# Another order of a recurrence step's pieces on TensorE

## The chip, the core and the metric

The kernel runs on one core of a Trainium2 chip. The metric is the device time of one execution in microseconds (us); a median over runs is given beside the time of the one execution that the profiler recorded. TensorE does the matrix products, VectorE, ScalarE (ACT) and GpSimd the elementwise work, SyncE (SP) issues the DMAs.

## The reference, cut to what matters

One step of a hybrid decoder layer over 1040 prompt rows (16 meta rows in front) and 64 sample rows. The input projection feeds two branches; the RWKV branch, whose work the change reorders, is a recurrence over time:

```python
def _rwkv7_step(S, inp):
    r, w, k, v, kk, a = inp
    sa = jnp.einsum('bhvk,bhk->bhv', S, -kk)
    S = S * w[:, :, None, :] + sa[..., None] * (kk * a)[:, :, None, :] + v[..., None] * k[:, :, None, :]
    return S, jnp.einsum('bhvk,bhk->bhv', S, r)

z = _rms_norm(x, lp['pre1']) @ lp['w_in']            # columns of the RWKV branch, the mLSTM branch, the gates
S_T, y = lax.scan(_rwkv7_step, S0, (r, decay, k, v, kk, a))
merged = ga * (ya @ p_a) + gb * (yb @ p_b)
h = x + _rms_norm(merged @ w_out, post1)
out = h + _rms_norm(jnp.square(jax.nn.relu(_rms_norm(h, pre2) @ w_ff_up)) @ w_ff_down, post2)
```

All products are in float32, the large ones as three products of rounded halves (hi*hi, hi*lo, lo*hi).

## The kernel before

The recurrence is computed in chunks of 64 rows. Four pairs of heads (j) times six groups (g) of three chunks make 24 steps; the last group of a pair holds two prompt chunks and the 64 sample rows. A group passes through four stages, one step each, so that in step i stage a works on group i, stage b on i-1, stage c on i-2 and stage d on i-3. Each stage is a generator that is cut into pieces by `yield`:

- Stage a (lines 637 to 757, six pieces) prepares the chunk: norms and gates (L651 to L667), the scaled keys (L673 to L702, on VectorE, ScalarE and GpSimd), the product L708 with X1, nd and its round trip through DRAM (L716 to L721, NR), values (L726, L727), the product L738 with MB, and bonus and gate (L746 to L756).
- Stage b (six pieces) inverts a triangular matrix. Its first piece is VectorE's alone: a chain of fifteen rounds of a product and a sum on small tiles (L766, L768), which reads NR, and then XC (L770). Pieces two to six each begin with a small product on TensorE (L778, L784, L794, L801, L807) and end with VectorE's reading of it (L780, L786, L796, L803; L811 with ScalarE's L810).
- Stage c (five pieces, seven with the sample rows) carries the state. Piece one forms GH and MR (L820 to L832). Pieces two, three and four multiply a chunk's GH with the state into pS, which has a single PSUM bank, and VectorE scales it into the next state St (L894); the chunk's output product follows one piece later. Piece five copies the output (L912). With the sample rows the products of L859 to L922 are added, and an order's entries 'e' call two more pieces.
- Stage d (four pieces) normalizes the output: a small product (L623, L946), eight Newton operations on VectorE (`newton`, lines 172 to 184), then scaling and the store.

TensorE also computes the input projection for later work in blocks of 72 matmuls (L283, L285, L287; three column tiles of 414, 414 and 276), the fill. `run_step` (L962) writes TensorE's order: it walks through a list of (stage, weight), calls that stage's next piece, and then pulls so many fill matmuls that their count follows the sum of the weights; a step's units are 72, or 144 in the last group of the first three head pairs. Entries of stages that have no work in a step are dropped with their weights. What stays of a stage at the end is run out, with two fill matmuls behind each piece.

`ORDER` serves 19 full steps (three of them with the sample rows, entries 'e' counted), three without stage a at the start of a new pair of heads, and three at the end. `ORDER_B` serves step 1 alone, in which only stages a and b have work, and `ORDER_A` step 0 and stage a by itself at a new pair. TensorE's order is kept as written (`manual_schedule`, L565). The order on VectorE, ScalarE, GpSimd and SyncE is laid down by the framework's planner when the program is built, from the order of the program and from when it takes an operation to be ready; each of these engines then runs its own queue in that order.

Of the kernel before, what the change touches and what calls it, by code (L numbers as in the profile page):

```python
# [102 lines left out]
def tile_hybrid_trunk_step(ctx, tc, x_prompt, x_sample, st_S, st_shift, st_C, st_n, st_m, st_conv,  # L103
# [210 lines left out]
    def blocks(n):  # L314
        drain()
        for _ in range(n):
            pull(1)
            drain()
# [56 lines left out]
    with banks(s=4, m=2), ExitStack() as st:  # L375
# [91 lines left out]
        with tc.manual_schedule(engines={mybir.EngineType.Activation, mybir.EngineType.PE}):  # L467
# [5 lines left out]
            for i in range(9):  # L473
# [6 lines left out]
                if i in CASTS:  # L480
                    b = first[len(w_first)]
# [473 lines left out]
        dma(out=yscr[j][:, GC * g + y0 - 64:GC * g + GC - 64], in_=yo[:, :ny])  # L955
        yield

    ORDER = (('c', 7), ('a', 0), ('c', 7), ('b', 3), ('c', 6), ('a', 6), ('c', 0), ('c', 9), ('d', 1), ('a', 0), ('b', 8), ('b', 4), ('b', 3), ('d', 0), ('a', 0), ('b', 6), ('e', 4), ('d', 0), ('e', 10), ('a', 0), ('b', 8), ('a', 0))
    ORDER_B = (('c', 6), ('a', 0), ('p', 68), ('b', 0), ('c', 15), ('c', 6), ('d', 0), ('a', 11), ('c', 0), ('c', 2), ('b', 0), ('a', 0), ('b', 7), ('b', 1), ('b', 4), ('d', 0), ('a', 0), ('e', 4), ('a', 0), ('b', 15), ('a', 1), ('e', 10), ('d', 0))
    ORDER_A = (('a', 39), ('a', 3), ('a', 6), ('a', 0), ('a', 7), ('a', 13))  # L960

    def run_step(gens, order, units, smp=False):  # L962
        todo = [(x, w) for x, w in order if x in gens or x == "p" or (x == "e" and smp)]
        tot = sum(w for _, w in todo)
        did = acc_ = 0
        for x, w in todo:
            next(gens.get("c" if x == "e" else x, iter(())), None)
            acc_ += w
            want = units * acc_ // tot
            pull(want - did)  # L970
            did = want
        for x in "dcba":
            for _ in gens.get(x, ()):
                pull(2)
# [9 lines left out]
    for i in range(NS + 3):  # L984
# [5 lines left out]
        if i >= NS:  # L990
            run_step(gens, ORDER, 72 * (i < NS + 2), i == NS + 1)
            continue
        j, g = steps[i]
        if g == 0 and j:
            mix_all()
            queue.pop(0)
            run_step(gens, ORDER, 72)
            blocks(0)
            mix_all()
            queue.pop(0)  # L1000
            run_step({"a": stage_a(j, g, sts[j, g])}, ORDER_A, 72 * FILLS[0])
        else:
            gens["a"] = stage_a(j, g, sts[j, g])
            run_step(gens, ORDER_A if i == 0 else ORDER_B if i == 1 else ORDER, 72 * (FILLS[g] + (g == 5) * (1 if j == 3 else 2)), g == 1 and j > 0)
            while g == 5 and j < 3 and (live or queue[0]):
# [174 lines left out]
    for c0 in (0, 5):  # L1180
        ps = sbank()
        for c in range(c0, c0 + 5):
            a, n = CH[c]
            nc.tensor.transpose(ps[:n, 68 * (c - c0):68 * (c - c0) + 68], E2[:, a:a + n], ident[:68, :68])
        for c in range(c0, c0 + 5):
            a, n = CH[c]
# [354 lines left out]
    for m in range(8):  # L1541
# [7 lines left out]
        for a, n in O_TILES:  # L1549
# [4 lines left out]
            e = min(a + n, 1024)  # L1554
# [466 lines left out]
```

## Time and profile before

| | |
|---|---|
| runs | 2024.83, 2026.06, 2026.5 us; median 2026.06 |
| profiled execution | 2024.88 us, its span 2023.0 us |
| TensorE matmuls busy | 1928.6 us (95%) |
| TensorE weight loads busy | 1747.6 us (86%) |
| VectorE busy | 1292.1 us (64%) |
| ScalarE, GpSimd busy | 795.6 us, 619.2 us |
| the 24 recurrence steps | about 84 to 840 us of the span |

The profile is that of one execution. Its engines are PE (TensorE's matmuls), PEld (its weight loads), DVE (VectorE), ACT (ScalarE), POOL (GpSimd) and SP (SyncE). A matmul's duration holds its way through the array, so that matmuls overlap: two fill matmuls start about 0.18 us apart and last 0.35 us each. An idle time in brackets is counted from the modelled end of the one before.

### The profile page before, as it was taken

The page shows a single profiled execution, that of the slowest core. Times are in us where ns is not written, and L with a number is a line of the kernel's source. Part 1 is how long each engine was busy: PE and PEld are TensorE (multiplying, and loading weights), DVE is VectorE, ACT ScalarE, POOL GpSimd, SP SyncE. Part 2 cuts the span into 40 slices and gives each one's busy share as a digit, 9 for nine tenths or more (in the row PEclk, how much of TensorE's full clock was granted, in tenths as well). Part 3 has the DMA queues.
Part 4 walks back from the last instruction along what each step waited for, and adds up shares of the span by engine and source line. Part 5 has one row for each costly group of instructions (what it writes and reads, how often), then busy time and mean ns, then how long its engine had stood idle before and what let it go on. Part 6 is the DMA issues. An engine that isn't in the chain of part 4 may idle for free. (4 is left out here: it accounts for less than half of the span.)

```text
span 2023.0 us, 35063 instructions
## 1 busy us (share of the span) xinstructions
PE 1928.6 (95%) x13163; PEld 1747.6 (86%) x13163; DVE 1292.1 (64%) x3464; ACT 795.6 (39%) x1841; POOL 619.2 (31%) x816
## 2 busy tenths in 40 slices
PE   8999999999999999999899998999999999999996
PEld 8988888888888888999788886999999978888875
DVE  6367668867767787487766539764334326666658
ACT  6434334433434343355565324453443442222212
POOL 3311221221122112252533305444444312222225
PEclk9989999999999999889999999999999999999998
DMA  5122112212111122132666614322333362222212
GB/s 162 53 69 72 52 46 68 66 47 69 64 54 58 58 66 71 49 110 82 221 193 201 214 56 149 119 94 87 103 114 97 123 226 86 87 87 88 95 59 88
DMA packets 163193, 197.43 MB, mean 98 GB/s; under 512 B 22060, under 2 KB 125542, under 8 KB 163024
## 3 DMA queue, kind: packets, MB, share of 16 engines
q1 hardware_dynamic: 163024, 195.19, 30.0%
q8 instruction: 104, 1.70, 0.3%
q14 instruction: 65, 0.53, 0.1%
HBM read 139.80 MB, written 55.10 MB: 96 GB/s over the span
## 5 line engine op out<-in xcount | busy, mean ns | idle before, releaser
L207 POOL TENSOR_TENSOR lo<-raw,hi 128x128 fp32r<-128x128 f32 (+1 forms) x528 | 327.4, 654 | 807.8 <-ACT hi L200 762.5
L283 PE MATMUL g<-u,hi 128*128 128x414 f32 (+4 forms) x1120 | 382.7, 342 | 1.9 <-ACT gst L533 1.1
L287 PE MATMUL g<-u,lo 128*128 128x414 f32 (+4 forms) x1120 | 383.6, 342 | 0.0
L285 PE MATMUL g<-u,hi 128*128 128x414 f32 (+4 forms) x1120 | 381.5, 341 | 0.0
L1930 DVE TENSOR_TENSOR ACC<-g,ACC 128x512 f32<-128x512 f32 x234 | 159.2, 689 | 118.0 <-PE g L221 118.0
L283 PEld LDWEIGHTS g<-u,hi 128*128 128x128 f32 x1120 | 215.9, 193 | 7.4 <-issue 1.5
L287 PEld LDWEIGHTS g<-u,lo 128*128 128x128 f32 x1120 | 215.9, 193 | 5.1 <-POOL lo L207 0.3
L285 PEld LDWEIGHTS g<-u,hi 128*128 128x128 f32 x1120 | 215.7, 193 | 3.8 <-issue 0.2
L219 PE MATMUL g<-hi,ah 128*128 128x512 f32 (+1 forms) x515 | 202.8, 394 | 2.4 <-ACT ah L1886 2.4
L220 PE MATMUL g<-lo,ah 128*128 128x512 f32 (+1 forms) x515 | 203.4, 395 | 0.9 <-POOL lo L207 0.8
L221 PE MATMUL g<-hi,ah 128*128 128x512 f32 (+1 forms) x515 | 202.7, 394 | 0.4 <-DVE ah L1887 0.2
L200 ACT CAST hi<-raw 128x1024 fp32r<-128x1024 f32 x98 | 102.5, 1047 | 68.4 <-PE g L285 18.5
L1886 ACT CAST ah<-hr 128x1088 fp32r<-128x1088 f32 x32 | 34.0, 1103 | 220.5 <-PE g L220 217.0
L1823 PE MATMUL g<-T,op 128*128 128x272 f32 x416 | 120.3, 289 | 0.0
L1821 PE MATMUL g<-T,op 128*128 128x272 f32 x416 | 120.2, 289 | 0.0
L1822 PE MATMUL g<-T,op 128*128 128x272 f32 x416 | 120.0, 289 | 0.0
L219 PEld LDWEIGHTS g<-hi,ah 128*128 128x128 f32 x515 | 97.0, 188 | 25.7 <-ACT ah L1886 2.8
L220 PEld LDWEIGHTS g<-lo,ah 128*128 128x128 f32 x515 | 96.9, 188 | 24.4 <-POOL lo L207 2.2
L221 PEld LDWEIGHTS g<-hi,ah 128*128 128x128 f32 x515 | 97.0, 188 | 23.6 <-DVE ah L1887 1.2
L766 DVE TENSOR_TENSOR tmp<-NR,x 128x45 f32<-128x45 f32 (+4 forms) x360 | 83.4, 232 | 28.6 <-DMA NR<-ndr 21.4
L1782 POOL TENSOR_TENSOR op<-S,op 128x512 fp32r<-128x512 f32 x52 | 68.3, 1314 | 83.0 <-ACT op L1781 79.5
L1823 PE MATMUL g<-mg,op 128*128 128x272 f32 x312 | 89.9, 288 | 0.0
(543 smaller groups left out, 4525.2 us busy)
## 6 DMA issues: line engine op xcount, KB each, us to landing
raw<-in_w_in_dram SPq DMA_DIRECT2D x44, 512.0 KB
hr<-hD SPq DMA_DIRECT2D x32, 544.0 KB
raw<-in_w_ff_up_dram SPq DMA_DIRECT2D x32, 512.0 KB
raw<-in_w_ff_down_dram SPq DMA_DIRECT2D x32, 512.0 KB
hD<-H SPq DMA_DIRECT2D x52, 272.0 KB
NR<-ndr SPq DMA_DIRECT2D x24, 384.0 KB
gscr<-gst SPq DMA_DIRECT2D x16, 544.0 KB
xt<-in_x_prompt_dram SPq DMA_DIRECT2D x15, 512.0 KB
```

Source lines behind the costliest of these rows:

```text
L200: nc.scalar.copy(out=hi, in_=raw)
L207: PO.tensor_tensor(out=lo[:, k:k + step], in0=raw[:, k:k + step], in1=hi[:, k:k + step].bitcast(F32), op=ALU.subtract)
L219: mm(ps, lhsT=wh, rhs=xh, start=(i == 0), stop=False)
L220: mm(ps, lhsT=wh, rhs=xl, start=False, stop=False)
L221: mm(ps, lhsT=wl, rhs=xh, start=False, stop=(i == last))
L283: mm(ps, lhsT=hi[:, k], rhs=xh, start=(k == 0), stop=False)
L285: mm(ps, lhsT=hi[:, k], rhs=xl, start=False, stop=False)
L287: mm(ps, lhsT=lo[:, k], rhs=xh, start=False, stop=(k == 7))
L1821: mm(o, lhsT=op[:, 0, k], rhs=xh, start=(k == 0), stop=False)
L1822: mm(o, lhsT=op[:, 0, k], rhs=xl, start=False, stop=False)
L1823: mm(o, lhsT=op[:, 1, k], rhs=xh, start=False, stop=(k == 3))
L1930: V.tensor_tensor(out=ACC[:, i, cs], in0=ps, in1=ACC[:, i, cs], op=ALU.add)
```

## The change

It replaces the three lists. In `ORDER` the first two pieces of stage c stand at the head, and stage a's first piece, which stood between them, comes after the second; stage b's first piece follows it. The weights move: more fill stands between the second, third and fourth piece of stage c and between the fourth and the fifth, less behind stage c's first and fifth piece and behind stage b's second. Stage b's fifth piece comes after stage a's fourth and fifth and stage d's third, with no fill between these and stage b's fourth; stage b's sixth comes right after its fifth's fill. `ORDER_B` and `ORDER_A` keep their sequence; three weights of `ORDER_B` change (of which one entry, ('b', 16), counts in the step that uses it).

```diff
-    ORDER = (('c', 7), ('a', 0), ('c', 7), ('b', 3), ('c', 6), ('a', 6), ('c', 0), ('c', 9), ('d', 1), ('a', 0), ('b', 8), ('b', 4), ('b', 3), ('d', 0), ('a', 0), ('b', 6), ('e', 4), ('d', 0), ('e', 10), ('a', 0), ('b', 8), ('a', 0))
-    ORDER_B = (('c', 6), ('a', 0), ('p', 68), ('b', 0), ('c', 15), ('c', 6), ('d', 0), ('a', 11), ('c', 0), ('c', 2), ('b', 0), ('a', 0), ('b', 7), ('b', 1), ('b', 4), ('d', 0), ('a', 0), ('e', 4), ('a', 0), ('b', 15), ('a', 1), ('e', 10), ('d', 0))
-    ORDER_A = (('a', 39), ('a', 3), ('a', 6), ('a', 0), ('a', 7), ('a', 13))
+    ORDER = (('c', 5), ('c', 7), ('a', 3), ('b', 5), ('c', 10), ('a', 4), ('c', 6), ('c', 0), ('d', 1), ('a', 0), ('b', 6), ('b', 4), ('b', 0), ('d', 0), ('e', 7), ('a', 0), ('d', 0), ('a', 0), ('e', 6), ('b', 6), ('b', 7), ('a', 0),)
+    ORDER_B = (('c', 6), ('a', 0), ('p', 68), ('b', 0), ('c', 15), ('c', 6), ('d', 0), ('a', 11), ('c', 0), ('c', 0), ('b', 0), ('a', 0), ('b', 7), ('b', 1), ('b', 4), ('d', 0), ('a', 0), ('e', 3), ('a', 0), ('b', 16), ('a', 1), ('e', 10), ('d', 0),)
+    ORDER_A = (('a', 39), ('a', 3), ('a', 6), ('a', 0), ('a', 7), ('a', 13),)
```

In what follows a1 to a6, b1 to b6, c1 to c5 and d1 to d4 are the pieces of the stages.

## Rows read from the trace of the kernel before

**Rows 1.** The page's first part: busy us (share of the span) and instructions by engine.
```profile
PE 1928.6 (95%) x13163; PEld 1747.6 (86%) x13163; DVE 1292.1 (64%) x3464; ACT 795.6 (39%) x1841; POOL 619.2 (31%) x816
```

**Rows 2.** TensorE's waits, 126 to 840 us: waiter, releaser, us in total, times, longest.
```profile
PE c L630 <- DVE St L894: 25.0, 29, 2.3
PE b L807 <- DVE bdx L803: 3.8, 3, 1.5
```

**Rows 3.** TensorE's timeline: start, duration, instruction, [idle before]; head of one step.
```profile
362.15 0.83 PE L820 MATMUL s<-MB,ATb 128*128 128x128 f32 x6
...
364.07 0.42 PE L283 MATMUL g<-u,hi 128*128 128x398 f32 x1
...
365.42 0.28 PE L654 MATMUL a<-Ct,sq 128*128 128x2 f32 x2
...
366.38 0.33 PE L630 MATMUL c<-Vs,GH 64*64 64x65 f32 x4
...
366.76 0.46 PE L285 MATMUL g<-u,hi 128*128 128x398 f32 x1
...
368.68 0.34 PE L287 MATMUL g<-u,lo 128*128 128x398 f32 x1
370.45 0.33 PE L630 MATMUL c<-Vs,GH 64*64 64x65 f32 x4 [1.43 <-DVE St L894]
```

**Rows 4.** VectorE's timeline in the same step.
```profile
361.78 0.23 DVE L766 TENSOR_TENSOR tmp<-NR,x 128x45 f32<-128x45 f32 x1
...
368.06 0.16 DVE L658 TENSOR_SCALAR rho<-a 64x2 f32<-64x2 f32 x1
...
370.12 0.28 DVE L894 TENSOR_SCALAR St<-c,LM 128x65 f32<-128x65 f32 x1
...
373.05 0.35 DVE L770 TENSOR_TENSOR XC<-x,Ct 128x192 f32<-128x192 f32 x1
```

**Rows 5.** Stretches: us, busy (x count) by engine, granted clock, DMA share, GB/s.
```profile
362.10:387.80 25.70, 24.25 (x230) 22.38 (x229) 20.26 (x80) 10.48 (x31) 5.13 (x12) 1.00 0.23 77
...
765.90:769.30 3.40, 3.40 (x11) 2.93 (x9) 3.37 (x11) 2.62 (x8) 1.98 (x3) 0.51 0.01 2
```

**Rows 6.** TensorE's timeline, stage b's pieces of the same step.
```profile
377.74 0.54 PE L778 MATMUL b<-XC,X 64*64 64x32 f32 x12
...
380.78 0.38 PE L794 MATMUL b<-XC,X 64*32 64x32 f32 x12
...
382.34 0.38 PE L801 MATMUL b<-QZ,XT 64*32 64x32 f32 x12
382.65 0.40 PE L283 MATMUL g<-u,hi 128*128 128x276 f32 x1
...
383.51 0.83 PE L738 MATMUL a<-RB,bdb 128*128 128x128 f32 x6
384.18 0.83 PE L807 MATMUL b<-X,bdx 128*128 128x128 f32 x6
```

**Rows 7.** VectorE's timeline beside these pieces.
```profile
381.98 0.36 DVE L946 TENSOR_SCALAR sqd<-c 128x192 f32<-128x192 f32 x1 [0.26 <-PE c L623]
...
382.66 0.36 DVE L174 SCALAR_TENSOR_TENSOR nt<-dg 128x192 f32<-128x192 f32 x1
382.94 0.53 DVE L803 COPY bdx<-b 32x96 f32<-32x96 f32 x2
```

**Rows 8.** VectorE's and TensorE's timelines in a step of 144 units.
```profile
232.99 0.23 DVE L766 TENSOR_TENSOR tmp<-NR,x 128x45 f32<-128x45 f32 x1 [3.70 <-DMA NR<-ndr]
...
234.89 0.57 PE L807 MATMUL b<-X,bdx 128*128 128x128 f32 x3 [1.24 <-DVE bdx L803]
```

**Rows 9.** TensorE's timeline, c2 in a step without stage a.
```profile
243.32 0.33 PE L630 MATMUL c<-Vs,GH 64*64 64x65 f32 x4 [0.89 <-ACT GH L830]
```

**Rows 10.** GpSimd's and VectorE's timelines at the head of the step of rows 3.
```profile
362.28 3.42 POOL L207 TENSOR_TENSOR lo<-raw,hi 128x128 fp32r<-128x128 f32 x8 [15.06 <-ACT hi L200]
...
364.11 0.38 DVE L766 TENSOR_TENSOR tmp<-NR,x 128x36 f32<-128x36 f32 x1
```

## The prediction

> **What bounds the kernel now.** I read four views, in this order. First the page's busy line [rows 1]: TensorE is busy for 1928.6 of 2023.0 us, so about 94 us of the span are its idle time, and an order of the same work can give back only idle time and lost clock. The change touches only the recurrence steps, from about 120 to 840 us. Second, TensorE's waits in that stretch [rows 2]: one line carries most of them, 25.0 us in 29 waits of a pS matmul (L630) for the VectorE copy St (L894); the next is 3.8 us in three waits of the last piece of stage b (L807) for L803. Third, one step in order of time [rows 3]: stage c begins at 362.15, its second piece (c2) at 366.38, eleven fill matmuls follow from 366.76, and the third piece (c3) starts at 370.45 after 1.43 us of idleness. No other wait of that step comes near. Fourth, VectorE in the same step [rows 4]: St of c2 runs only at 370.12 and ends at 370.40, 3.4 us after c2 gave way to the fill (366.76). In VectorE's queue it stands inside stage b's small chain (L766, L768), which began at 361.78 and isn't through before L770 at 373.05, and behind stage a's rho operations (the first at 368.06). So a step is TensorE's own work plus a wait for VectorE that recurs at one place, between c2 and c3.
>
> A second loss hangs on it. Behind three of these waits (near 472, 657 and 766 us) the granted clock is half for 3.4 us [rows 5], of which one of the three is shown: 11 matmuls in 3.40 us, where [rows 3] has eleven starts within 1.92 us. That is 1.4 us lost each time.
>
> **Where the fill goes.** Each list entry is a piece and a weight; a step of 72 fill matmuls is dealt out by weight. A full step without the sample part sums to 68 before and 64 after, so a weight is worth 1.06 and 1.125 fills.
> - c1 to c2: 7.4 fills and stage a's first piece before, 5.6 fills after, and no a1.
> - c2 to c3: 10.6 fills before (11 in the rows); after 7+3+5=15 weights, 16.9 fills, and a1.
> - c3 to c4: 12.7 before, 15.75 after; c4 to c5: none before, 6.75 after.
> - b2 to b3: 8.5 before, 6.75 after; b3 to b4: 4.2 and 4.5; b4 to b5: 3.2 fills before, none after, but a4 and a5 lie there.
> - b5 to b6: 6.4 fills and a5 before, 6.75 fills alone after.
>
> **The wait for St.** c1 lasts 1.92 us (362.15 to 364.07), the seven fills after it 1.35 (0.19 each, edge included), a1 0.96, c2 0.38 [rows 3]. After the change c2 stands at 1.92+5.6*0.19=3.0 us from c1's start (4.23 before), and c3 at 3.0+0.38+16.9*0.19+0.96=7.6, with 0.2 for one more edge 7.8. St ended at 370.40, that is 8.25, before. So even if VectorE's queue doesn't change, 1.43 us becomes 0.5. But St can be ready 1.2 us earlier and the rho operations (a1) now come after it, so St moves up by more than 0.5 us where the planner takes what is ready in program order. I take the wait as gone in ordinary steps. In the three sample steps and where c2 is late I leave 2.0 us in all: 25.0 becomes 2.0, gain **23.0**; bounds 15 (queue unmoved: 0.5 in 13 other steps, 1.1 in the three sample steps, where 15 weights are 14 fills) and 25. With the waits their half-clock stretches go: 3*1.4, gain **4.2** (bounds 0, if other short stalls bring them, and 4.2).
>
> **The end of stage b.** In the step at 377 to 385 us b5 starts at 382.34, the fill behind it at 382.65, six fills take 0.86, a5 0.67, and b6 starts at 384.18 [rows 6], 1.84 after b5. After: 0.31+6.75*0.143=1.28 us after b5. What b6 needs, the two copies of L803, ended at 383.47 [rows 7], 1.13 after b5. So slack falls from 0.7 to about 0.1 us. VectorE is at that moment in the newton operations of stage d (0.36 us each), and d's third piece now stands ahead of b5 in the program. One more newton operation ahead of L803 gives 0.3 us, none gives nothing, all of them far more (a rival, below). The row nearest is [rows 7], where L803 came in after three operations of that chain, with no more than one in its way; I take 0.1 us in 19 steps, **+2.0**, bounds 0 and 6.
>
> In the three steps with double fill b6 already waits, 1.24 us in the one shown [rows 8], 3.8 in all: L803 is queued behind a first L766 that itself waited 3.70 us for the DMA of NR, which starts from a3. There a3 to b5 shrinks from 15 weights to 10 (of 2.1 and 2.25 fills), so d2's and b5's VectorE work is ready earlier while NR's landing stays tied to a3: the copies should pass L766. Gain **3.5**, bounds 0 and 3.8.
>
> **Small terms.** a1 split from c2, c4 from c5, and a5 joined to b4's group make 11 groups of small matmuls where there were 10 (13 for 11 in sample steps), 22 more switches between fill and small matmuls. The trace shows none alone; it costs no less than nothing and no more than the 0.31 us from b5's start to the next fill [rows 6]. Fills ahead of a1 take 0.19 with an edge; I take 0.15, **+3.3**, bounds 0 and 6.8. In the three steps without stage a the time from c1 to c2 loses 1.8 fills, 0.3 us; c2 waited there for ACT's GH once, 0.89 us [rows 9]; **+0.9**, bounds 0 and 3. The second list (one step) moves a single fill, the third only gains a comma: 0.
>
> What is late next: a3 stands 46 fills into the step instead of 41, so 0.9 us closer to the next c1. Before, stage b's chain was through at 373.40 (L770) and b2 began at 377.74 [rows 4, 6]: 4.3 us of cover, of which at most 0.9 and the removed 1.4 go. 2 us stay, so I cost this at nothing.
>
> **Sum.** -23.0-4.2+2.0-3.5+3.3+0.9=-24.5 us on the profiled execution's 2024.9 (span 2023.0 and 1.9 around it): 2000.4. That execution lies 1.2 under the median of the runs, so 2001.6, given as **2001.5**. Its own range, by the bounds above, 1993 to 2011.
>
> **Rivals.**
> - *The queue doesn't follow.* VectorE's order is the planner's, not this list's. If St stays behind the same rounds, the gain of the first term is 15 and the sample steps keep two half-clock stretches: 24.5-8-2.8=13.7, so 2012.4. For it: St was placed that late although it is earlier in the program than the chain. Against: c2 moves 1.2 us. Chance 0.17.
> - *Slower: newton first.* If all eight newton operations run before L803, TensorE pays at b6. L946 began 1.2 us after b4 [rows 6, 7]; without three fills (0.43) it would end about 1.3 after b4, eight operations of 0.36 with their gaps 3.0 later, L803's 0.53 more: 4.85 us. b6 would stand at 3.1 (b4 to b5 1.56 less 0.43 plus a5's 0.67, then 1.28). 1.75 us in 19 steps is 33, in place of 2: 2001.6+31=2033. It decides from 1.4 us a step. Against: chains are interleaved in [rows 7], not run whole. Chance 0.09.
> - *VectorE becomes the bound.* It is busy 20.26 us of 25.70 in this step [rows 5], and the step would shrink to about 24.3, 83%. While GpSimd splits weights (3.42 us from 362.28), a chain operation takes 0.38 us [rows 10], against 0.23 just before [rows 4]. If the burst covered 24 of the chain's 30 operations, the chain would grow by 3.6 us, use up the 2 us of cover and let b2 wait 1.6 us in 16 steps, 26 in all: 2027. Against: the burst begins with the block, as before. Chance 0.06. The Trainium skill (GPSIMD Engine Reference, 1. Specifications) says that GpSimd shares its SBUF interfaces with VectorE and that instructions with two SBUF inputs contend, which speaks against packing the head of the step; the trace agrees (0.38 us), but only within the burst.
> - *It doesn't do what it says.* New small waits replace the old one for one, no difference: 2024 to 2028. For it: a step's waits moved between lines would leave TensorE's idle time as it is; against: the cover that grows (c2 to c4) lies where 25.0 us are and the cover that shrinks has slack. Chance 0.05.
>
> **How the numbers follow.** The forecast has 0.63. Faster by over 0.2% (about what a measurement of this kernel can tell from none): 0.63+0.17=0.80, and 0.02 of the third rival, 0.82; within 0.2%: 0.04 of the third and 0.05 of the fourth, 0.09; slower 0.09. The range must leave out no more than 0.2: from 1991 (bounds that all fall well) to 2018 (the first rival with its margin), which leaves out the last cases and a little at either end.
>
> **What would show it.** Right: the line of L630 for St falls from 25.0 to a few us; St's VectorE start moves ahead of the rho operations; ordinary steps last some 24 us instead of 25 to 26; half-clock stretches near 472, 657 and 766 are gone; L807's wait for L803 is spread thin, under 3 us. Wrong: L807 waits in every step (newton first), L778 waits for XC (VectorE bound), or L630 for St keeps over 8 us (queue unmoved).

## The result and the profile after

The changed kernel takes 2003.09 us (median of 1997.38, 2002.57, 2003.62 and 2005.67) where the kernel before took 2025.44 on the same chip: a ratio of 0.9891, 95% interval 0.9863 to 0.992. A second set of runs gave 2002.95 us and 0.9899 (0.9883 to 0.9915). The prediction of 2001.5 us (1991 to 2018) was right. The profiled execution took 2005.67 us.

The page's first part of the changed kernel, which answers to [rows 1]:
```profile
span 2003.8 us, 35069 instructions
...
PE 1931.3 (96%) x13163; PEld 1744.9 (87%) x13163; DVE 1296.9 (65%) x3464; ACT 795.8 (40%) x1841; POOL 621.0 (31%) x816
```
The instruction counts of the five engines are those of before, and TensorE is 2.7 us busier, in a span 19.2 us shorter. The gain is idle time and lost clock, as said. The Trainium skill (Perfetto Trace Analysis, Identifying the Most-Contended Engine) calls the busy share of matmuls no good measure of how near a kernel is to its roofline, since pipelined matmuls look smaller in the trace. This case bears out that the share says little: it went from 95% to 96%, a version below takes out another 12 us of time, and joining c4 to c5 lowers the busy time of a step's same matmuls from 24.71 to 24.35 us.

TensorE's waits of the changed kernel from 126 to 840 us (waiter, releaser, us in total, times, longest), which answer to [rows 2]:
```profile
PE b L807 <- DVE bdx L803: 4.2, 8, 0.8
PE c L922 <- DVE smpD L874: 2.1, 3, 0.7
PE s L860 <- POOL smpD L855: 1.6, 1, 1.6
PE b L801 <- DVE QZ L796: 1.2, 4, 0.3
PE c L630 <- DVE GH L829: 0.9, 1, 0.9
...
PE c L630 <- DVE St L894: 0.4, 2, 0.2
```
The line that carried 25.0 us is down to 0.4. All lines of this view sum to 35.2 us before and 10.8 after. What is left heads a new list: b6 (L807) for L803 is now eight waits of at most 0.8 us instead of three of up to 1.5, and b5 (L801) waits four times, which it didn't before.

One ordinary step of the changed kernel (72 units, with stage a, without the sample rows; c1 begins at 351.61), TensorE's timeline, which answers to [rows 3] and [rows 6]: c1, c2, a1, c3, c4, c5, a3, b2, b5, b6, and the next c1.
```profile
351.61 0.83 PE L820 MATMUL s<-MB,ATb 128*128 128x128 f32 x6
...
354.61 0.33 PE L630 MATMUL c<-Vs,GH 64*64 64x65 f32 x4
...
356.55 0.28 PE L654 MATMUL a<-Ct,sq 128*128 128x2 f32 x2
...
359.21 0.33 PE L630 MATMUL c<-Vs,GH 64*64 64x65 f32 x4
...
363.07 0.33 PE L630 MATMUL c<-Vs,GH 64*64 64x65 f32 x4
...
365.01 0.33 PE L630 MATMUL s<-MR,Vs 64*64 64x64 f32 x4
...
365.63 1.14 PE L708 MATMUL a<-KB,bda 128*128 128x192 f32 x6
...
366.69 0.54 PE L778 MATMUL b<-XC,X 64*64 64x32 f32 x12
...
371.26 0.38 PE L801 MATMUL b<-QZ,XT 64*32 64x32 f32 x12
...
373.22 0.91 PE L807 MATMUL b<-X,bdx 128*128 128x128 f32 x6 [0.49 <-DVE bdx L803]
...
376.80 0.83 PE L820 MATMUL s<-MB,ATb 128*128 128x128 f32 x6
```
And VectorE in it, which answers to [rows 4] and [rows 7]: St of c2, the first rho operation, St of c3, and the operations around b6's copies.
```profile
357.02 0.28 DVE L894 TENSOR_SCALAR St<-c,LM 128x65 f32<-128x65 f32 x1
...
358.72 0.16 DVE L658 TENSOR_SCALAR rho<-a 64x2 f32<-64x2 f32 x1
...
360.83 0.36 DVE L770 TENSOR_TENSOR XC<-x,Ct 128x192 f32<-128x192 f32 x1
...
362.73 0.28 DVE L894 TENSOR_SCALAR St<-c,LM 128x65 f32<-128x65 f32 x1
...
372.28 0.24 DVE L803 COPY bdx<-b 32x96 f32<-32x96 f32 x1
372.45 0.34 DVE L174 SCALAR_TENSOR_TENSOR nt<-dg 128x192 f32<-128x192 f32 x1
372.82 0.26 DVE L803 COPY bdx<-b 32x96 f32<-32x96 f32 x1
```
Four readings. c2 stands 3.00 us behind c1 (forecast 3.0) and c3 7.60 (forecast 7.8). St of c2 ends 5.69 behind c1, where it ended at 8.25, ahead of the rho operations instead of behind them. The next St ends at 363.01 and c4 starts at 363.07: the second St has 0.06 us of slack, no more. And a newton operation (L174) now splits the pair of copies of L803; b6 starts 1.96 us behind b5, where 1.28 was forecast.

Where the time went: the recurrence ends where L1151 first starts (duration min/median/max, first and last start). Before, in the changed kernel, and in the changed kernel's second profile:
```profile
L1151 PE MATMUL g<-u,wh x48: 285/348/358, 844.1 to 852.0; 128*100 128x414 f32 x32, 128*100 128x276 f32 x16
```
```profile
L1151 PE MATMUL g<-u,wh x48: 284/347/358, 819.3 to 827.2; 128*100 128x414 f32 x32, 128*100 128x276 f32 x16
```
```profile
L1151 PE MATMUL g<-u,wh x48: 284/347/358, 819.4 to 827.3; 128*100 128x414 f32 x32, 128*100 128x276 f32 x16
```
So 24.8 us are won by then (the forecast's sum was 24.5), nearly all of them, 24.1, between the first and the last step's c1. By the end of this execution 5.6 of them are gone. There is more time at half the granted clock behind the recurrence: 46.5 us here, 30.5 in the execution of before. One of them, in the first profile of the changed kernel and at the same place of the second (stretch, length, busy us and counts of PE, PEld, DVE, ACT, POOL, clock, DMA share, GB/s):
```profile
1075.00:1082.50 7.50, 6.79 (x23) 6.01 (x23) 2.79 (x6) 2.44 (x3) 0.76 (x2) 0.54 0.76 245
```
```profile
1075.00:1082.50 7.50, 7.07 (x40) 6.59 (x40) 2.05 (x4) 1.05 (x1) 3.45 (x9) 1.00 0.94 316
```
The granted clock is 0.54 (the level of 1.2 GHz nearly throughout) against 1.00 (2.4 GHz), with 23 matmuls against 40, in the same program. The second execution's span is 2000.4 us, so that 3.4 of the 5.6 us belong to the execution and not to the order. The forecast had set nothing aside for what comes behind the recurrence.

### The profile page after: what moved, and what is told of

Same layout as the page of the kernel before. It is cut to its first block, busy times and chain, and to the rows that moved or that the text cites. A ratio compares the mean times of both kernels' runs of the same rounds, so it can differ in the third digit from the quotient of the medians.

```text
span 2003.8 us, 35069 instructions
## 1 busy us (share of the span) xinstructions
PE 1931.3 (96%) x13163; PEld 1744.9 (87%) x13163; DVE 1296.9 (65%) x3464; ACT 795.8 (40%) x1841; POOL 621.0 (31%) x816
## 5 line engine op out<-in xcount | busy, mean ns | idle before, releaser
L287 PE MATMUL g<-u,lo 128*128 128x414 f32 (+4 forms) x1120 | 378.2, 338 | 0.0
L283 PEld LDWEIGHTS g<-u,hi 128*128 128x128 f32 x1120 | 213.3, 190 | 7.1 <-ACT gst L533 1.5
L285 PEld LDWEIGHTS g<-u,hi 128*128 128x128 f32 x1120 | 213.5, 191 | 4.5 <-issue 0.2
L220 PEld LDWEIGHTS g<-lo,ah 128*128 128x128 f32 x515 | 97.2, 189 | 24.6 <-POOL lo L207 2.2
L221 PEld LDWEIGHTS g<-hi,ah 128*128 128x128 f32 x515 | 97.3, 189 | 23.9 <-DVE ah L1887 1.2
L766 DVE TENSOR_TENSOR tmp<-NR,x 128x45 f32<-128x45 f32 (+4 forms) x360 | 82.3, 229 | 23.0 <-DMA NR<-ndr 13.7
```

The source lines that it names most:

```text
L220: mm(ps, lhsT=wh, rhs=xl, start=False, stop=False)
L221: mm(ps, lhsT=wl, rhs=xh, start=False, stop=(i == last))
L283: mm(ps, lhsT=hi[:, k], rhs=xh, start=(k == 0), stop=False)
L285: mm(ps, lhsT=hi[:, k], rhs=xl, start=False, stop=False)
L287: mm(ps, lhsT=lo[:, k], rhs=xh, start=False, stop=(k == 7))
```

## The experiments

Each kernel's median, its ratio to the kernel before with the interval, the start of L1151 in its profile (844.1 before; L1153 and L1155 in the last two kernels, which have more lines), and how long its granted clock was at half from 60 us to that start (37.5 us before, summed over the stretches). The runs come from several chips and times, at which the kernel before took 2025.2 to 2027.6 us; the ratios allow for that, the medians don't.

| kernel | us | ratio | L1151 at | half clock |
|---|---|---|---|---|
| the change (two sets) | 2003.1, 2003.0 | 0.989, 0.990 | 819.3, 819.4 | 23.9 |
| head alone | 2012.9 | 0.9953 (0.9934, 0.9971) | 829.9 | 17.1 |
| end of the list alone | 2015.8 | 0.9961 (0.9947, 0.9975) | 834.2 | 27.3 |
| one entry moved | 2019.5 | 0.9975 (0.9961, 0.9988) | 835.9 | 30.7 |
| c4 with c5 | 1994.8 | 0.9836 (0.9816, 0.9856) | 808.5 | 3.4 |
| a5 moved back | 1999.9 | 0.9868 (0.9842, 0.9893) | 814.6 | 13.7 |
| d3 moved back | 2011.6 | 0.9921 (0.99, 0.9941) | 829.8 | 27.3 |
| three repairs | 2029.4 | 1.0018 (0.9999, 1.0036) | 835.4 | 23.9 |
| c4 with c5, a1 with c2 | 2006.2 | 0.9906 (0.9883, 0.9929) | 818.3 | 13.7 |
| c4 with c5, a5 back | 1997.0 | 0.9864 (0.984, 0.9887) | 811.8 | 17.1 |
| the same, sample steps apart | 1993.6 | 0.9847 (0.9826, 0.9868) | 810.8 | 17.1 |
| three lists | 1990.6 | 0.9816 (0.9795, 0.9837) | 806.9 | 17.1 |

**The head of the list alone**, on the kernel before:
```diff
-('c', 7), ('a', 0), ('c', 7), ('b', 3), ('c', 6), ('a', 6), ('c', 0), ('c', 9), ('d', 1), ('a', 0),
+('c', 5), ('c', 7), ('a', 3), ('b', 5), ('c', 10), ('a', 4), ('c', 6), ('c', 0), ('d', 1), ('a', 0),
...
```


> The kernel before with only the first ten entries of the list changed (the two recurrence pieces at the head, a1 behind them, the head's new weights); the last twelve as before. Theory (the head carries the gain): the waits of L630 for St between 126 and 840 us fall from 25.0 to under 2 us, the wait of b6 (L807) stays at the three double-fill steps, about 3 to 4 us, and the extra group of small matmuls costs its 0.4 us a step as in the changed kernel; about 1997 to 2003 us, that is as fast as the changed kernel or up to 6 us faster. Rival (the end of the list carries it): the St waits keep over 10 us, 2015 us or more.


**Its end alone**, on the kernel before:
```diff
...
-('b', 8), ('b', 4), ('b', 3), ('d', 0), ('a', 0), ('b', 6), ('e', 4), ('d', 0), ('e', 10), ('a', 0), ('b', 8), ('a', 0)
+('b', 6), ('b', 4), ('b', 0), ('d', 0), ('e', 7), ('a', 0), ('d', 0), ('a', 0), ('e', 6), ('b', 6), ('b', 7), ('a', 0)
```


> The kernel before with only the last twelve entries changed (b5 and b6 behind a4, a5 and d3). Theory (the head carries the gain): the St waits stay at 20 to 27 us, since the chain of L766 and the rho operations of a1 still stand ahead of St, the wait of b6 appears in ordinary steps as in the changed kernel (0.28 to 0.64 us each), 2022 to 2031 us, no gain. Rival (the end of the list carries it): 2012 us or less.


Both times missed: neither half carries the gain (the St line and b6's wait with the end alone are about as expected). The recurrence ends 14.2 us earlier with the head and 9.9 with the end; that these add up to 24.1, where the change wins 24.8, is luck. From the first c1 to the last the head wins 15.3, the end 2.1 and the change 24.1 us. The rest of the end's is 2.8 us ahead of the first c1, where TensorE's order is that of before, and 5.0 in the last step; its profile has 3.4 and 10.2 us less at half clock there. TensorE's waits, 126 to 840 us, with the head alone and with the end alone:
```profile
PE c L630 <- DVE St L894: 6.7, 11, 1.2
...
PE b L807 <- DVE bdx L803: 1.4, 2, 0.8
```
```profile
PE c L630 <- DVE St L894: 19.8, 19, 2.9
PE b L807 <- DVE bdx L803: 4.3, 8, 0.8
```
A reason that the halves need each other is that weights are shares. The head's list sums to 70 for a full step, the change's to 64, so the ten weights behind c3, with a2's four, are 14.4 fills instead of 15.75. Of the 6.7 us that stay, 5.8 are c4's wait for the second St. The other way round, the shorter end (62 in all) gives every head piece more fill: in each 144-unit step St waits of 0.7 to 1.1 us go, and b6's wait there with them. Those steps fall from 38.3, 37.7 and 37.7 us to 35.2, 35.4 and 34.6, 8.4 us in all; the other steps lose 6.4 of that again. Its ordinary steps are up to 0.8 us longer than before, one 1.4, and one step with the sample rows, with 10.2 us at half clock instead of 3.4, is 3.2 longer.

**One entry moved**: a1 behind c2, all weights as before.
```diff
-('c', 7), ('a', 0), ('c', 7), ('b', 3),
+('c', 7), ('c', 7), ('a', 0), ('b', 3),
...
```


> The kernel before with a single entry moved: a1 goes behind c2; every weight stays. Between c2 and c3 only a1's 0.96 us is added, the same eleven fills stay. Theory A (St moves up in VectorE's queue, because c2 comes about 1.2 us earlier and a1's rho operations now come after it): St ends 5.5 to 6.3 us behind the start of c1 instead of 8.25, the waits of L630 for St fall under 4 us in all, 2000 to 2007 us. Theory B (VectorE's queue stays as it was, only the cover grew): St still ends near 8.25, c3 would stand at about 7.0 and wait 1.2 us in each step, 2019 to 2026 us.


TensorE's timeline in its step from 360.62 (c2, c3, c4), then VectorE's (St of c2, the first rho operation, St of c3):
```profile
363.98 0.33 PE L630 MATMUL c<-Vs,GH 64*64 64x65 f32 x4
...
367.46 0.33 PE L630 MATMUL c<-Vs,GH 64*64 64x65 f32 x4
...
371.35 0.33 PE L630 MATMUL c<-Vs,GH 64*64 64x65 f32 x4 [0.78 <-DVE St L894]
```
```profile
366.62 0.28 DVE L894 TENSOR_SCALAR St<-c,LM 128x65 f32<-128x65 f32 x1
368.07 0.16 DVE L658 TENSOR_SCALAR rho<-a 64x2 f32<-64x2 f32 x1
...
371.01 0.28 DVE L894 TENSOR_SCALAR St<-c,LM 128x65 f32<-128x65 f32 x1
```
Theory A is right in its mechanism: St ends 6.28 us behind c1 (5.5 to 6.3 expected, 8.25 if the queue had stayed), and c3 waits for nothing in this step. Its time is wrong by 12 us or more, since the wait moved one piece on: c4 is now there 0.78 us ahead of its St. The St line keeps 15.1 us, 11.1 of them at c4. The time alone, 2019.5 us, would have spoken for theory B, whose mechanism the rows rule out. So the order of c2 and a1 clears c3, and the weights behind c3 clear c4; the change needs both.

**The changed kernel again**, for a second profile.

> The changed kernel a second time, for a second profile of it. If the 5.6 us that its first profile lost again behind the recurrence (24.8 us ahead of the kernel before at L1151, 19.2 ahead at the end) belong to the order, the same half-clock stretches near 967 to 973, 1075 to 1082 and 1601 to 1604 us come back. If they belong to the single execution, the recurrence ends again at 819 to 820 us and the stretches behind it differ from the first profile's.


The recurrence ended at 819.4, and the stretch at 1075 to 1082 is absent, as the rows above show. Those from 966 and from 1598 us (1601 in the first) came in both executions. So each theory has a part: 3.4 of the 5.6 us lost behind the recurrence are the execution's, 2.2 are not accounted for by it.

**c4 joined to c5**, in the changed kernel:
```diff
-('c', 6), ('c', 0), ('d', 1),
+('c', 0), ('c', 6), ('d', 1),
...
```


> The changed kernel with stage c's fifth piece joined to its fourth again (weights 0 and 6 in place of 6 and 0, no fill between them); all else stays. In an ordinary step of the kernel with the head alone the 12 switches into small matmuls cost about 0.33 us more than in the one with a single entry moved, whose only other difference in that place is c4 and c5 apart. Theory 1 (the split of c4 and c5 is what made the step grow): 0.3 us less in each of about 20 steps, 5 to 7 us below the changed kernel, 1996 to 1998 us against its 2003. Theory 2 (the split of a1 from c2 did it): no difference, 2001 to 2005.


The same step in the two kernels, the change and this one (columns as above):
```profile
351.60:376.80 25.20, 24.71 (x229) 22.37 (x229) 21.32 (x80) 10.50 (x29) 5.34 (x13) 1.00 0.23 78
```
```profile
348.08:372.92 24.84, 24.35 (x230) 22.23 (x230) 21.51 (x80) 10.51 (x29) 5.33 (x13) 1.00 0.24 79
```
25.20 becomes 24.84, and the two other kinds of ordinary step go from 24.69 to 24.34 and from 24.29 to 23.96. Theory 1: a group of small matmuls costs 0.35 us where it is c5 behind six fills; 16 of the steps are 0.28 to 0.37 us shorter. The recurrence ends 10.8 us earlier, more than the 5.4 us that these add up to. From the first c1 to the last the steps win 4.9, since in two of those with the sample rows L872 now waits 1.7 us for VectorE's L861. In the last step 3.9 are won, where a stretch of 6.8 us at half clock didn't come. And 1.9 lie ahead of the first c1, where the stretch at half clock lasted 3.4 us instead of 10.2, though the same 762 matmuls stand there in the same order in both kernels. Why it is shorter is open: the last kernel below has that order, too, and 10.2 us again.

**a5 between b5 and b6 again**, and **d3 behind b6 again**, each alone in the changed kernel:
```diff
-('a', 0), ('d', 0), ('a', 0), ('e', 6), ('b', 6), ('b', 7), ('a', 0)
+('a', 0), ('d', 0), ('e', 6), ('b', 6), ('a', 0), ('b', 7), ('a', 0)
```


> The changed kernel with a5 between b5 and b6 again, in one group with b6; d3 stays ahead of b5. Theory (b6 lacks cover: a5's 0.67 us and the fill behind b5 must outlast VectorE's copies of L803): the 6.8 us that b6 starts late in all steps fall under 1.5 us, and a5 no longer joins b4's group, 5 to 8 us below the changed kernel, 1995 to 1998. Rival (the newton operation of stage d between the two copies is what counts; in VectorE's queue one, L179, still stands there): half or more of the lateness of b6 stays, 1999 to 2003.


```diff
-('a', 0), ('d', 0), ('a', 0), ('e', 6), ('b', 6), ('b', 7), ('a', 0)
+('a', 0), ('a', 0), ('e', 6), ('b', 6), ('d', 0), ('b', 7), ('a', 0)
```


> The changed kernel with d3 (the newton operations) behind b5 and b6 again, a5 where the change put it. In VectorE's queue the two copies of L803 then stand side by side and two newton operations fewer stand ahead of them. If the newton operations cause the lateness of b6: it falls from 6.8 us to under 2.5, 4 to 6 us below the changed kernel, 1997 to 1999. If the lost cover does: it keeps over 4 us, 2000 to 2004.


Counted by the spacing of starts over all steps, b6 was 6.8 us late in the changed kernel. With a5 back it is 0.06, with d3 back 1.1. So it takes both to make b6 late: the newton operations in VectorE's queue and the lost 0.67 us of a5. With a5 back the recurrence ends 4.7 us earlier than in the changed kernel; the interval of the ratio overlaps the change's, so that the gain in time is not shown. With d3 back it ends 10.5 us later (the median is 8.5 us higher, the ratio by 0.002 to 0.003, with intervals that just overlap), from two places that the expectation didn't have. First, in this kernel TensorE's waits show a new line, and its timeline the place:
```profile
PE a L664 <- ACT gg L750: 2.8, 3, 1.1
```
```profile
309.06 0.36 PE L664 MATMUL a<-Z,wuh 128*128 128x192 f32 x1 [1.07 <-ACT gg L750]
```
and ScalarE's timeline says what L750 waited for, in this kernel and in the changed one:
```profile
308.69 0.32 ACT L750 COPY gg<-a 128x192 f32<-128x192 f32 x1 [3.57 <-DVE yo L954]
```
```profile
303.47 0.32 ACT L750 COPY gg<-a 128x192 f32<-128x192 f32 x1 [0.39 <-DVE bv L749]
```
gg has three buffers, and L954, the end of stage d, is the last to read one. With the newton operations later, L954 is later (it ends at 308.66 instead of 298.89), gg is written 5.2 us later, and the next group's a1 (L664) finds its PSUM bank not yet read. Second, the last two products of stage d (L623) follow 45 fill matmuls instead of 6 and 7 behind the last L935, and the work behind the last step's c1 lasts 46.5 us instead of 39.8. Why the edit moved them there I did not find.

**Three repairs at once**: a1 with c2, c4 with c5, a5 back, d3 back.
```diff
-('c', 5), ('c', 7), ('a', 3), ('b', 5), ('c', 10), ('a', 4), ('c', 6), ('c', 0), ('d', 1),
+('c', 5), ('c', 0), ('a', 10), ('b', 5), ('c', 10), ('a', 4), ('c', 0), ('c', 6), ('d', 1),
...
-('a', 0), ('d', 0), ('a', 0), ('e', 6), ('b', 6), ('b', 7), ('a', 0)
+('a', 0), ('e', 6), ('b', 6), ('d', 0), ('a', 0), ('b', 7), ('a', 0)
```


> Three repairs at once: a1 joined to c2 and c5 to c4, a5 between b5 and b6, d3 behind b6. If the costs add up: 6 us for c4 with c5, 7 us for b6, nothing for a1 with c2; 1988 to 1992 us. A rival: with fifteen weights less evenly spread the next St comes late for c4, which would bring a line of 5 us or more for L630 on St back: 1994 to 2000.


Far outside both: no gain over the kernel before. The rival's wait came (the St line), its time didn't. The waits:
```profile
PE c L630 <- DVE St L894: 12.2, 16, 1.2
PE a L664 <- ACT gg L750: 5.6, 3, 1.9
```
The second line is the gg chain of the run above. The first was isolated by taking **c4 with c5 and a1 with c2** without the rest:
```diff
-('c', 5), ('c', 7), ('a', 3), ('b', 5), ('c', 10), ('a', 4), ('c', 6), ('c', 0), ('d', 1),
+('c', 5), ('c', 0), ('a', 10), ('b', 5), ('c', 10), ('a', 4), ('c', 0), ('c', 6), ('d', 1),
...
```


> The kernel with c4 and c5 joined, and in addition a1 joined to c2 again (behind it, weights 0 and 10 in place of 7 and 3); all else as in that one, which took 1994.8 us. If a1's own place costs nothing, as the step with a single entry moved says (its step grew by 0.0 us although it has one switch more): within 3 us of it, 1992 to 1998. If a switch costs 0.3 us wherever it is: 5 to 7 us faster, 1988 to 1990. If a1 directly behind c2 is too early for what it needs (the kernel with three repairs had 5.6 us in three waits of L664 for ScalarE's L750, and c4's wait for St back): slower, 2002 to 2012.


```profile
PE c L630 <- DVE St L894: 8.8, 16, 1.1
```
That is the third expectation's time (2006.2 us, 11.3 above c4 with c5 alone), but by another wait than L664: a1's rho operations reach VectorE 1.4 us earlier (357.33 instead of 358.72 in a step that begins at the same 351.61), St of c3 ends at 363.68 instead of 363.01, and c4, which had 0.06 us of slack, waits 0.64:
```profile
357.33 0.16 DVE L658 TENSOR_SCALAR rho<-a 64x2 f32<-64x2 f32 x1
...
363.74 0.33 PE L630 MATMUL c<-Vs,GH 64*64 64x65 f32 x4 [0.64 <-DVE St L894]
```
The fill that the change put between c2 and a1 thus does work of its own.

**c4 with c5 and a5 back**, then **the same with a list of its own for the sample steps**, where c4 and c5 stay apart:
```diff
+    ORDER_S = (('c', 5), ('c', 7), ('a', 3), ('b', 5), ('c', 10), ('a', 4), ('c', 6), ('c', 0), ('d', 1),
...
+        order = ORDER_S if smp else order
```


> The two edits that each made the changed kernel faster, together: c4 joined to c5, and a5 between b5 and b6. Alone they ended the recurrence 10.8 and 4.7 us earlier. If the costs are independent, 15 us earlier than the changed kernel, 803 to 806 us for the end of the recurrence, and 1989 to 1992 us in all. If the removed waits were only cover for each other (St of c3 late for c4, which waited 1.5 us in all with a5 moved), 1993 to 1997.

> The same, but the steps with the sample rows keep c4 and c5 apart (a list of its own for them), because with both joined L872 waited there for VectorE's L861, 3.4 us in two waits. If that wait is what joining costs in these steps: gone, 2 to 4 us faster than the kernel with both edits in every step, 1986 to 1989 us. If something else in the sample steps takes its place (L860 for GpSimd's L855, L922 for L874): no difference.


The edits don't add up: 1997.0 us, no better than c4 with c5 alone. Ordinary steps did get faster (23.7, 24.0 and 24.3 us against 24.3, 24.0 and 24.8), but the 144-unit steps went from 35.2, 34.7 and 34.7 to 35.3, 35.2 and 35.6 us. Part of that is a new wait, 0.9 us in two of them: with a5 later, a6 waits for ScalarE's L742, which reads a5's product. The two steps from 231 us took another 4.1 us more, with 6.8 us at half clock that c4 with c5 alone doesn't have there. The row of a6 from a 144-unit step with a5 back alone:
```profile
409.85 0.65 PE L755 MATMUL a<-Cl,bdL 128*128 128x128 f32 x4 [0.57 <-ACT MB L742]
```
In the sample steps L872's line fell from 1.6 to 0.5 us; 1993.6 against 1997.0 us is in that direction, with intervals that overlap.

**Three lists**: both edits in 72-unit steps with stage a, a5 as the change has it in the 144-unit steps and in those without stage a, c4 and c5 apart with the sample rows.
```diff
+        if order is ORDER:
+            order = ORDER_S if smp else ORDER_D if units == 144 or "a" not in gens else ORDER
```


> Three lists, each where it did best: c4 with c5 and a5 between b5 and b6 in the 72-unit steps with stage a; c4 with c5 but a5 where the change put it in the 144-unit steps and in those without stage a (with a5 later a6, L755, waited there 0.6 to 0.9 us for ScalarE's L742); c4 and c5 apart with the sample rows. If the waits belong to the steps: ordinary steps 23.7, 24.0 and 24.3 us, 144-unit steps 34.7 us, no line of L872 for L861 over 1 us, recurrence through at 801 to 804 us, 1987 to 1991 us in all. If VectorE's and ScalarE's queues, which are laid out for the whole program, carry a wait from one kind of step into the next (c2 for GH, 3 to 4 us in the two kernels with a5 moved): 1992 to 1996, no better than c4 joined to c5 alone.


Two of its steps, an ordinary one and one of 144 units:
```profile
349.10:373.34 24.24, 24.17 (x230) 22.19 (x229) 20.51 (x79) 10.51 (x30) 5.12 (x12) 1.00 0.24 79
373.34:408.00 34.66, 34.66 (x292) 32.54 (x290) 26.10 (x98) 14.52 (x40) 10.73 (x20) 1.00 0.20 56
```
The steps are as the first theory said (but for the first of 144 units, 35.2 us), and the time (1990.6 us) lies in its range; the recurrence ended 3 us later than it said, with the first half-clock stretch at 10.2 us. From the first c1 to the last its steps win 6.4 us over c4 with c5 alone. It is the fastest version found, 1.84% below the kernel before, but its interval overlaps that of c4 with c5 alone (1994.8 us), which is a single exchange of two weights.

## Why the prediction was right, point by point

- **The wait for St**, forecast -23.0: 25.0 became 0.4, -24.6. The queue did follow, which the run with one entry moved shows by itself (6.28 us against 8.25); the first rival falls. But the step was incomplete: it put all 29 waits between c2 and c3. Only 22 of them are c3's; c4 had the other 7, and once c3 is cleared c4 waits longer. I counted the fill between c3 and c4 and gave it no price; without it 6.7 us (the head alone) to 15.1 us (one entry moved) of the line stay.
- **Where the steps gain**: ordinary steps were to last some 24 us instead of 25 to 26, and that sign didn't come. In the second pair of heads the three took 23.9, 24.8 and 25.7 us before and 24.7, 24.3 and 25.2 after; from c1 to c1 all thirteen together win 2.3 us. Their 12.6 us of waits for St are gone, but b6 is 6.6 us late in them, c5 apart from c4 costs 3.4, and c2 waits once for GH (0.9). The rest of the 24.1 us lies in the other steps: 8.2 in the three of 144 units, 3.8 in the three without stage a at the start of a pair, 10.5 in the three with the sample rows; the one before the last loses 0.7.
- **Half-clock stretches**, forecast -4.2: up to the start of L1151 37.5 us at half clock became 23.9. By the forecast's own 1.4 us lost of 3.4, 13.6 us less is 5.6 us, an estimate. Of the three named stretches, those at 657 and 766 us are gone; the step that had the one at 472, 9.6 us behind its c1, still has one of the same length 12.8 us behind it, where TensorE waited only 0.2 us for St. Others come and go with the order and without it.
- **b6 in ordinary steps**, forecast +2.0 at 0.1 us a step: mis-sized. It came 0.28 us late in steps with 128 columns of stage d and 0.64 in those with 192, 6.8 in all by the spacing of starts, 4.2 by the view of waits (which shows only what exceeds the modelled end of the matmul before). I had allowed for a newton operation ahead of L803, not for one between its two copies. Putting back either cause removed it. The full rival, all eight operations first, did not happen.
- **b6 in the 144-unit steps**, forecast -3.5: b6 stood 1.2 to 1.7 us late and now at most 0.09. Right.
- **Groups of small matmuls**, forecast +3.3 at 0.15 us each: mis-sized and put on the wrong pieces. What the waits (-24.4) and the clock (-5.6) leave of -24.8 is +5.2. Of that, 2.1 are b6's, since by the spacing of starts it is later than the waits show (6.8 against 4.2, before 4.3 against 3.8). The run with one entry moved has a1 apart at no cost; c4 and c5 joined give back 5.4 in 16 steps. These two are 2.3 more than the remainder, so that the account doesn't close to better than that. Joining a5 to b4's group saved nothing that shows.
- **Steps without stage a**, forecast +0.9 for c2: its wait in those steps is gone (one of 0.9 us for GH stands in an ordinary step). Instead b5 comes 0.38 us late for L796 in four of them, now that b4, d2 and b5 stand together with no fill. Also unforeseen is L860's wait of 1.6 us in the last step.
- **VectorE as the bound**: no. Its busy time in the step is 21.32 of 25.20 us, XC (L770) is through at 361.19 and b2 starts at 366.69. Nothing waits for XC.

So that the sum fits (-24.5 against -24.8 at the end of the recurrence) is luck: two terms that were too small by some 4 us together were paid by the St wait and the clock, which gave more. The forecast's own range of 1993 to 2011 wasn't the sum of its bounds either: all the bad ones together (15 won by the wait for St, 15.8 lost elsewhere) come to 2027.

## What to carry to other kernels

In a list dealt out by weights, a weight is a share: price every stretch of the list after a change of any entry, and ask of each wait that is removed which piece waits for the same engine next. Here a moved piece mattered by when it put its work into another engine's queue more than by the matmuls it covered, and a piece must be followed through buffers too (here VectorE's late L954 held a buffer that stopped ScalarE and then TensorE). Repairs that each gain can cancel; combine them per kind of step, from the steps' own times. Those times also say where a gain lies: a sum of waits that went doesn't, since others can take their place in the same step.

## What was unexpected of the hardware

A change of shape between fill and small products is not one price: a1, two-column products, stands apart between fills at no cost, while c5 apart from c4 costs 0.35 us a step. And the stretch at half clock at the start of the recurrence lasted 10.2 us in nine of these thirteen kernels, 6.8 in two and 3.4 in two; what decides that stayed open. TensorE's order ahead of it doesn't: the changed kernel and the eight built on it have the same 762 matmuls there in the same order, and all three lengths.
